# Loading x and memory by features and moving 1/rms behind the product in a two-layer encoder trunk

## The chip, the cores and the metric

One core of one Trainium2 chip runs the whole program. The metric is device time in microseconds (us) of one execution; three executions of the kernel before are given.

## The reference, cut to what matters

Two sequences of 256 tokens with 1024 features each, and 256 memory tokens for each, go through two layers. All is fp32.

```python
def rms_norm(x, g):
    xf = x.astype(jnp.float32)
    y = xf * lax.rsqrt(jnp.mean(xf * xf, axis=-1, keepdims=True) + EPS)
    return (y * g.astype(jnp.float32)).astype(x.dtype)

# per layer i (0: differential attention, 1: dilated windows)
h = rms_norm(x, norm_mix[i])
kv = (rms_norm(mem, norm_mem[i]) @ w_mem_kv[i]).reshape(B, M, 2, X_HEADS, X_HEAD_DIM)
mk = rms_norm(kv[:, :, 0], xk_norm[i])
mv = kv[:, :, 1]
p = h @ w_in                     # queries, keys: rms_norm by head, rope; values as they are
xq = rms_norm(p[..., -X_WIDTH:].reshape(B, S, X_HEADS, X_HEAD_DIM), xq_norm[i])
cross = memory_attention(xq, mk, mv).reshape(B, S, X_WIDTH)
x = x + jnp.concatenate([mixed, cross], axis=-1) @ w_out
x = x + conv_ffn(rms_norm(x, norm_ffn[i]), w_up[i], conv_w[i], conv_b[i], w_down[i])
```

The root of the mean of squares is one number for each token (row of x or mem). It multiplies a whole row, so it commutes with the product by the weights. Behind the product, queries and keys are normed by head again, where a row's factor cancels but for the place of EPS.

## The kernel before, in words

The 512 tokens of the two sequences are four token tiles of 128 (NT = 4). A product of fp32 accuracy is made of three matmuls of rounded parts (`mm3`, lines 370 to 373: high by high, low weights by high, high weights by low), so each operand is split in a high part (`hh`, `wh`) and a low part (`hl`, `wl`). Weights come as units of 128 x 1024 (512 KB), in the order of a list: `w_loader` (L333) issues the load of each on SyncE's queue into one of three buffers `raw`, and `w_splitter` casts it on ACT (L348) and subtracts on DVE (L350) into one of six pairs `wh`, `wl`. `next_unit` hands the units to the products.

TensorE contracts over the partitions, so the operand must lie with features on partitions, and x and mem are loaded with tokens on them. `norm_transposed` (L391) therefore takes a token tile: ACT sums squares (L381), POOL adds EPS and takes the power -1/2 (L386, L387), then the first half of the row is multiplied by root and gain on DVE (L403) and the second by the root on ACT (L406) and by the gain on POOL (L408). Four TensorE transpositions of 128 x 128 a half (L415) go to a bank `tp`, and `evac_split` writes the high part on ACT (L428) and the low part on DVE (L430). `norm_h` does so for x, into `hh` and `hl`; `mem_tiles` for memory, into buffers `blk`. For layer 1 the transposition also permutes the tokens (`perm_fwd`).

`proj_first` (L526) is the first product, eight feature blocks by four token tiles for 512 columns, in the order of the list `FIRST`, which visits tiles as they come. It keeps one PSUM bank for each of the tiles (three `acc`, one `sc`). `fan_out` hands a finished bank's two halves to their posts: `qk_post` (L552: squares on ACT, sums on DVE, root on POOL by L572 and L573, scaling on DVE L577, rope on POOL L589 to L592, transposition on PE L605) or `v_post` (L618, a copy on ACT). The second product makes queries and keys of attention pair 0; then comes `mem_proj` (L678), keys and values of memory, token tile by token tile with all four weight units of it. Pairs' attention (`attn_a`) and the cross attention run beside the products. In layer 0's FFN, the down projection goes in two passes over column halves, and the memory product of layer 1 follows the second.

The order of instructions on each engine is not written out: every stage is a Python generator, and a planner in the program (`Sched`, with a cost for each operation and a queue of events by planned time) runs them and so issues the instructions in planned order. The chip then keeps each engine's order and waits by semaphores.

Two lines matter for the start. `load_x` is called with units X0_U and X1_U, and `start` sends x's first tile, then the gain, the identity, and the first unit.

Of the kernel before, what the change touches and what calls it, by code (L numbers as in the profile page):

```python
# [31 lines left out]
X0_U, X1_U = 1, 3  # L32
FIRST = [(0, 0), (1, 0), (0, 1), (1, 1), (2, 0), (2, 1), (0, 2), (1, 2), (2, 2), (3, 0), (3, 1), (3, 2), (0, 3), (1, 3), (2, 3), (3, 3)]
X_AT = (1, 2, 3)
# [227 lines left out]
def trunk_kernel(ctx: ExitStack, tc: tile.TileContext, io: dict, out: bass.AP):  # L262
# [7 lines left out]
    psum = ctx.enter_context(tc.tile_pool(name="psum", bufs=1, space=bass.MemoryType.PSUM))  # L270

# [31 lines left out]
    const.tile([128, 64], F32, name="spacer")  # L303
    X = const.tile([128, NT, D], F32, name="X")
    x_ready = []
    dma_t = [2.0]

    def dma(eng, out_, in_, nbytes):
        eng.dma_start(out_, in_)
        dma_t[0] += nbytes / 330e3  # L310
        return dma_t[0]

    mask = tail.tile([128, 2, 512], BF16, name="mask")
    subg = tail.tile([128, 128], F32, name="subg")
    convT = tail.tile([128, 2, 4, 2 * NFF], F32, name="convT")
# [17 lines left out]
    def w_loader():  # L333
        for u in range(len(plan)):
            for t in X_AT[0:1] if u == X0_U else X_AT[1:] if u == X1_U else ():
                load_x([t])
# [40 lines left out]
    def row_scale(src, h):  # L377

        ss = sm(2, "ss")
        for j in range(2):  # L380
            nc.scalar.activation(h[j].v, src[j], AF.Square, scale=1.0 / 32, accum_out=ss[:, j:j + 1])  # L381
            t = S.op("ACT", c_act(512, 0, 1))
        yield t
        rstd = sm(1, "rstd")
        s1 = sm(1, "s1")
        nc.gpsimd.tensor_scalar(s1, ss[:, 0:1], ss[:, 1:2], EPS, ALU.add, ALU.add)  # L386
        nc.gpsimd.tensor_tensor(rstd, s1, mhalf[:, 0:1], ALU.pow)  # L387
        yield S.op("POOL", 0.6)
        return rstd

    def norm_transposed(src, gkey, ident_, evac, src_done=None):  # L391

        g = gains[gkey]
        h = []
        for _ in range(2):
            b = yield from qn_s.get()
            h.append(b)
        rstd = yield from row_scale(src, h)
        finished = [S.event(), S.event()]

        def part(j):
            if j == 0:
                nc.vector.scalar_tensor_tensor(h[0].v, src[0], rstd, g[0].v, ALU.mult, ALU.mult)  # L403
                t = S.op("DVE", c_dve(512, 1))
            else:
                nc.scalar.activation(h[1].v, src[1], AF.Copy, scale=rstd)  # L406
                yield S.op("ACT", c_act(512, 1))
                nc.gpsimd.tensor_tensor(h[1].v, h[1].v, g[1].v, ALU.mult)  # L408
                t = S.op("POOL", c_pool(512))
            if src_done:  # L410
                src_done(j, t)
            yield t
            tp = yield from tp_s.get()
            for k in range(4):
                nc.tensor.transpose(tp.v[:, k * 128:k * 128 + 128], h[j].v[:, k * 128:k * 128 + 128], ident_)  # L415
                t = S.op("PE", T_PE)
            h[j].done(t)
            yield t
            yield from evac(j, tp)
            finished[j].set(S.now)  # L420

        S.spawn(part(1))
        S.spawn(part(0))
        for f in finished:
            yield f
# [13 lines left out]
    def norm_h(t, gkey, permuted, x_ev, h_ev):  # L439
# [18 lines left out]
        yield from norm_transposed([X[:, t, 0:512], X[:, t, 512:1024]], gkey, perm_fwd if permuted else ident, evac)  # L458
# [992 lines left out]
```

## Time and profile before

| | |
|---|---|
| executions | 1428.8, 1430.7, 1432.24 us (median 1430.7) |
| profiled execution | 1430.49 us |
| its span | 1428.5 us, granted clock 1.00 |
| TensorE busy | 1399.0 us, 98% |
| VectorE, ScalarE, GpSimd busy | 783.7, 622.1, 340.2 us |
| chain that ended last | PE 87%, POOL 5%, DVE 3% |
| DMA | 129.31 MB, mean 91 GB/s |

The span runs from the first to the last recorded instruction; the execution's time has a further 2 us around it. Busy times of matmuls are modelled: they are pipelined, so a row's duration (0.39 us at full speed) is longer than the distance to the next. Starts tell the pace. TensorE is the only engine that is nearly always busy; the places where it stands are what the lists of waits show.

### The profile page before, as it was taken

To read this page: it belongs to the slowest core of one execution; us is meant where nothing else is said; L and a number is where in the kernel's file an instruction comes from. 1 tells how busy PE (TensorE), PEld (TensorE's weight loads), DVE (VectorE), ACT (ScalarE), POOL (GpSimd) and SP (SyncE) were. 2 spreads that over 40 slices of the span, in tenths; PEclk is the share of its full clock that TensorE was granted. 3 is DMA by queue.
4 is the path that set the end of the run, shared out by engine and by line. 5 is a ranking of instruction groups with operands and counts; after the bars stand their busy time and mean duration, and the time that the engine had idled before them with its cause. 6 is when DMAs were issued, how large, how long until landed. Compare 5 with 4: busy or idle time off the path is not lost.

```text
span 1428.5 us, 18859 instructions
## 1 busy us (share of the span) xinstructions
PE 1399.0 (98%) x7168; PEld 1163.6 (81%) x7168; DVE 783.7 (55%) x1218; ACT 622.1 (44%) x1145; POOL 340.2 (24%) x652
## 2 busy tenths in 40 slices
PE   6999999999999999999999999999999999999999
PEld 4778788879888888878878888888889888888887
DVE  5576657876664366445664334344476663466353
ACT  5566555535442244244446534454454442243231
POOL 5834665121000000030164165445130000000000
PEclk9999999999999999999999999999999999999999
DMA  6421231123333333423221311222222323333221
GB/s 224 150 74 46 62 116 60 60 74 105 106 100 95 97 103 90 136 100 133 74 89 29 96 68 59 60 63 77 83 87 91 103 92 100 97 95 103 89 74 59
DMA packets 39258, 129.31 MB, mean 91 GB/s; under 512 B 4608, under 2 KB 5504, under 8 KB 39168
## 3 DMA queue, kind: packets, MB, share of 16 engines
q1 hardware_dynamic: 39168, 128.11, 28.6%
q8 instruction: 56, 0.92, 0.3%
q14 instruction: 34, 0.28, 0.1%
HBM read 126.00 MB, written 2.10 MB: 90 GB/s over the span
## 4 chain that ended last, share of the span: by engine, by line
PE 87%; POOL 5%; DVE 3%; issue 2%; DMA 2%; ACT 1%; SPq 0%; POOLq 0%; DVEq 0%; ACTq 0%
PE acc L371 17%; PE acc L373 17%; PE acc L372 17%; PE sc L371 7%; PE sc L372 7%; PE sc L373 7%; PE sc L784 3%; PE tp L707 2%; PE o L982 2%; POOL rstd L573 2%; PE tp L605 1%; DMA raw<-w 1%; PE o L371 1%; PE o L372 1%; PE o L373 1%
## 5 line engine op out<-in xcount | busy, mean ns | idle before, releaser
L350 DVE TENSOR_TENSOR wl<-raw,wh 128x1024 fp32r<-128x1024 f32 x220 | 273.7, 1247 | 244.9 <-ACT wh L348 243.7
L348 ACT CAST wh<-raw 128x1024 fp32r<-128x1024 f32 x220 | 231.2, 1053 | 369.7 <-PE sc L372 187.9
L371 PE MATMUL acc<-wh,hh 128*128 128x512 f32 (+1 forms) x536 | 216.6, 404 | 0.8 <-ACT hh L428 0.8
L373 PE MATMUL acc<-wh,hl 128*128 128x512 f32 (+1 forms) x536 | 203.7, 380 | 0.0
L372 PE MATMUL acc<-wl,hh 128*128 128x512 f32 (+1 forms) x536 | 203.4, 379 | 0.0
L371 PE MATMUL acc<-wh,blk 128*128 128x512 f32 x368 | 149.1, 405 | 0.0
L372 PE MATMUL acc<-wl,blk 128*128 128x512 f32 x368 | 143.6, 390 | 0.0
L373 PE MATMUL acc<-wh,blk 128*128 128x512 f32 x368 | 143.6, 390 | 0.0
L371 PE MATMUL acc<-hh,wh 128*128 128x512 f32 (+1 forms) x384 | 143.2, 373 | 0.0
L371 PE MATMUL sc<-hh,wh 128*128 128x512 f32 (+1 forms) x384 | 142.8, 372 | 0.0
L372 PE MATMUL acc<-hl,wh 128*128 128x512 f32 (+1 forms) x384 | 142.6, 371 | 0.0
L373 PE MATMUL sc<-hh,wl 128*128 128x512 f32 (+1 forms) x384 | 142.6, 371 | 0.0
L372 PE MATMUL sc<-hl,wh 128*128 128x512 f32 (+1 forms) x384 | 142.6, 371 | 0.0
L373 PE MATMUL acc<-hh,wl 128*128 128x512 f32 (+1 forms) x384 | 142.6, 371 | 0.0
L371 PEld LDWEIGHTS acc<-wh,hh 128*128 128x128 f32 x536 | 101.9, 190 | 20.7 <-issue 5.3
L373 PEld LDWEIGHTS acc<-wh,hl 128*128 128x128 f32 x536 | 101.2, 189 | 19.9 <-DVE hl L430 0.3
L372 PEld LDWEIGHTS acc<-wl,hh 128*128 128x128 f32 x536 | 101.7, 190 | 14.1 <-DVE wl L350 0.5
L386 POOL TENSOR_SCALAR s<-ss 128x1 f32<-128x1 f32 x24 | 11.4, 475 | 425.6 <-ACT qn L381 419.8
L573 POOL TENSOR_TENSOR rstd<-ss,mhalf 128x4 f32<-128x4 f32 x96 | 105.5, 1099 | 8.0
L567 DVE TENSOR_REDUCE ss<-sq 128x4 f32<-128x256 f32 x96 | 39.8, 415 | 88.0 <-ACT sq L564 87.6
L373 PEld LDWEIGHTS acc<-hh,wl 128*128 128x128 f32 x384 | 72.3, 188 | 12.6
L371 PEld LDWEIGHTS acc<-hh,wh 128*128 128x128 f32 x384 | 72.3, 188 | 12.5
(145 smaller groups left out, 2412.3 us busy)
## 6 DMA issues: line engine op xcount, KB each, us to landing
raw<-w SPq DMA_DIRECT2D x220, 512.0 KB, 3.6
blk<-mem SPq DMA_DIRECT2D x16, 256.0 KB, 6.6
y<-X SPq DMA_DIRECT2D x8, 256.0 KB, 2.0
X<-x SPq DMA_DIRECT2D x3, 512.0 KB, 9.7
blk<-norm_mix SPq DMA_DIRECT2D x4, 256.0 KB, 7.0
blk<-norm_mem SPq DMA_DIRECT2D x4, 256.0 KB, 5.5
blk<-norm_ffn SPq DMA_DIRECT2D x4, 256.0 KB, 5.1
X<-x SPq DMA_DIRECT2D x2, 256.0 KB, 3.2
```

The costliest lines, as they stand in the source:

```text
L348: nc.scalar.copy(hi.v, r.v)
L350: nc.vector.tensor_tensor(lo.v, r.v, hi.v.bitcast(F32), ALU.subtract)
L371: nc.tensor.matmul(out_, ah, bh, start=start, stop=False)
L372: nc.tensor.matmul(out_, ah, bl, start=False, stop=False)
L373: nc.tensor.matmul(out_, al, bh, start=False, stop=stop)
L386: nc.gpsimd.tensor_scalar(s1, ss[:, 0:1], ss[:, 1:2], EPS, ALU.add, ALU.add)
L567: nc.vector.tensor_reduce(ss, sq.v[:, 0:256].rearrange("p (a d) -> p a d", d=64), AX.X, ALU.add)
L573: nc.gpsimd.tensor_tensor(rstd, ss, mhalf[:, 0:4], ALU.pow)
L605: nc.tensor.transpose(tp.v[:, x * 128:x * 128 + 128], src[:, x % 2, b * 128:b * 128 + 128], ident)
L707: nc.tensor.transpose(tp.v[:, i * 128:i * 128 + 128], e.v[:, i * 128:i * 128 + 128], ident)
L784: nc.tensor.matmul(sc[h].v[:, c:c + n], q.v[half(h), tq], k.v[half(h), ks], start=True, stop=True)
L982: nc.tensor.matmul(o[:, t, h, :], eT.v[:, i * 128:i * 128 + 128], vt[s].v[:, c:c + 64], start=(i == 0), stop=(i == 3))
```

## The change

x of layer 0 and memory of both layers are also handed over transposed by the host (`xT`, `memT`: features on partitions) and loaded as eight blocks of 128 features by 512 tokens. The norm's gain is then one number a partition, `gT`, and goes into the split (`split_feature`): ACT multiplies and rounds the high part, DVE subtracts. No transposition is made there. x and mem are loaded by rows too, for the sums of squares alone; `row_stats` leaves for each token tile the root and EPS times (mean square + EPS), `nr`. The second is the EPS of the norm by head in `qk_post` (a pointer in place of a constant), the first scales values in `v_post`. For layer 1's x, whose tokens are permuted by the transposition, these numbers are written to DRAM and read back in the new order (`permuted_stats`), and `norm_h` multiplies by the gain alone, both halves on DVE. The other norms (before the FFNs) keep root and gain, both halves on DVE. `proj_first` goes feature by feature over the four token tiles, and for the last unit tile by tile.

```diff
@@ the split and the statistics @@
+    def permuted_stats(s):
+        for i in range(2):
+            yield here[2 * s + i]
+        for i in range(2):
+            nc.sync.dma_start(nrmd[s][128 * i:128 * i + 128, :], nrmx[:, 2 * s + i, :])
...
+        for j in range(2):
+            for y in range(2):
+                nc.sync.dma_start(nrms[64 * y:64 * y + 64, 2, 2 * s + j, :], rows[2 * j + y])
...
+    def row_stats(key, src, done=None):
+        ss = yield from mean_squares(src, done)
+        m = sm(1, "s1")
+        eps, rstd = nr[key]
+        if key[0] == "x1":
+            eps, rstd = nrmx[:, key[1], 0:1], nrmx[:, key[1], 1:2]
+        nc.gpsimd.tensor_scalar(m, ss[:, 0:1], ss[:, 1:2], EPS, ALU.add, ALU.add)
+        nc.gpsimd.tensor_scalar(eps, m, EPS, None, ALU.mult)
+        nc.gpsimd.tensor_tensor(rstd, m, mhalf[:, 0:1], ALU.pow)
...
+    def split_feature(raw, g, hi, lo):
+        nc.scalar.activation(hi, raw, AF.Copy, scale=g)
+        nc.vector.scalar_tensor_tensor(lo, raw, g, hi.bitcast(F32), ALU.mult, ALU.subtract)
@@ norm_h @@
+            if permuted:
+                nc.vector.tensor_tensor(h[j].v, src[j], g[j].v, ALU.mult)
+            else:
+                nc.vector.scalar_tensor_tensor(h[j].v, src[j], rstd, g[j].v, ALU.mult, ALU.mult)
@@ proj_first @@
-        for u, t in FIRST:
...
+        for u in range(4):
+            wh, wl, done = yield from next_unit(name, 2)
+            order = [(k, t) for k in range(2) for t in range(NT)]
+            for k, t in order if u < 3 else sorted(order, key=lambda x: x[1]):
+                kk = 2 * u + k
+                yield k_evs[kk]
...
+                if kk == KD - 1:
+                    fan_out(t, bks[t], posts)
@@ qk_post, v_post @@
+            yield nr_ev[key, t]
-            nc.gpsimd.tensor_scalar(ss, ss, 1.0 / 64, EPS, ALU.mult, ALU.add)
+            nc.gpsimd.tensor_scalar(ss, ss, 1.0 / 64, nr[key, t][0], ALU.mult, ALU.add)
-            nc.scalar.copy(vs[s].val.v[:, 256 * i:256 * i + 256], ps)
+            nc.scalar.activation(vs[s].val.v[:, 256 * i:256 * i + 256], ps, AF.Copy, scale=nr[key, t][1])
@@ mem_tiles, mem_proj @@
+        for k in range(KD):
+            raw = yield from blk.get()
+            nc.sync.dma_start(raw.v, io["memT"][:, k, :])
+            landed = S.now + 4.0
...
+            yield landed
+            yield from split_feature(raw.v, gT[:, 1 + 3 * l, k:k + 1], hi.v, lo.v)
...
+            if k == 1:
+                S.spawn(rows())
...
+                    yield mT[kk]
+                    hi, lo = mT[kk].val
@@ the start @@
+    with_unit = {1: [lambda: load_xT(2), lambda: load_xT(3)], 2: [lambda: load_xT(4), lambda: load_xT(5)],
+                 3: [lambda: load_xT(6), lambda: load_xT(7)],
+                 4: [lambda: S.spawn(setup())] + [lambda t=t: load_x(t) for t in range(2)],
+                 5: [lambda t=t: load_x(t) for t in range(2, 4)]}
...
+        nc.sync.dma_start(gT, io["gT"])
+        load_xT(0)
+        yield 0.001
+        load_xT(1)
```

The planner moves more than the diff says. First, the start of TensorE's queue (`acc`, `tp` are PSUM banks, the number behind a name is the allocation). Before:

```order
L415 MATMUL tp_128<-ident,qn_115 128x128 x4
L415 MATMUL tp_137<-ident,qn_116 128x128 x4
L371 MATMUL acc_159<-wh_107,hh 128x512
L372 MATMUL acc_159<-wl_108,hh 128x512
L373 MATMUL acc_159<-wh_107,hl 128x512
L371 MATMUL acc_159<-wh_107,hh 128x512
L372 MATMUL acc_159<-wl_108,hh 128x512
L373 MATMUL acc_159<-wh_107,hl 128x512
L415 MATMUL tp_170<-ident,qn_142 128x128 x4
```

After:

```order
L366 MATMUL acc_99<-wh_113,hh 128x512
L367 MATMUL acc_99<-wl_114,hh 128x512
L368 MATMUL acc_99<-wh_113,hl 128x512
L366 MATMUL acc_100<-wh_113,hh 128x512
L367 MATMUL acc_100<-wl_114,hh 128x512
L368 MATMUL acc_100<-wh_113,hl 128x512
L366 MATMUL acc_101<-wh_113,hh 128x512
L367 MATMUL acc_101<-wl_114,hh 128x512
L368 MATMUL acc_101<-wh_113,hl 128x512
```

The transpositions are gone, and each weight tile is used for all four token tiles in turn, where before one tile ran ahead with the features at hand.

Second, TensorE's queue in the first token tile of layer 0's memory product (its bank is `acc_808` before, `acc_730` after; `blk` are the split features; `sc`, `e`, `eT`, `o` are scores, weights, transposed weights and outputs of attention pair 0). Before:

```order
L415 MATMUL tp_814<-ident,qn_768 128x128 x4
L371 MATMUL acc_808<-wh_457,blk_618 128x512
L372 MATMUL acc_808<-wl_458,blk_618 128x512
L373 MATMUL acc_808<-wh_457,blk_619 128x512
L415 MATMUL tp_832<-ident,qn_769 128x128 x4
L371 MATMUL acc_808<-wh_474,blk_618 128x512
L372 MATMUL acc_808<-wl_475,blk_618 128x512
L373 MATMUL acc_808<-wh_474,blk_619 128x512
L371 MATMUL acc_808<-wh_474,blk_618 128x512
```

After, from feature 5's three matmuls to feature 6's first; right above it stand feature 4's three matmuls, eight transpositions of queries (L644) and four scores (L813):

```order
L366 MATMUL acc_730<-wh_683,blk_767 128x512
L367 MATMUL acc_730<-wl_684,blk_767 128x512
L368 MATMUL acc_730<-wh_683,blk_768 128x512
L813 MATMUL sc_839<-blk_785,blk_587 128x256
L813 MATMUL sc_852<-blk_785,blk_587 128x256
L813 MATMUL sc_839<-blk_797,blk_614 128x256
L813 MATMUL sc_852<-blk_797,blk_614 128x256
L736 MATMUL tp_858<-ident,e_825 128x128 x2
L736 MATMUL tp_863<-ident,e_828 128x128 x2
L914 MATMUL o_815<-blk_508,eT_857 128x128 x2
L914 MATMUL o_815<-blk_508,eT_862 128x128 x2
L366 MATMUL acc_730<-wh_699,blk_818 128x512
```

Scores, transpositions of weights and outputs of pair 0, which stood among the matmuls of its later tiles and behind, now stand between the features of its first tile.

Third, SyncE's queue ahead of layer 1's memory product (`raw` is a weight unit, `memT` a feature block, `mem` half a tile by rows). Before:

```order
L323 DMA blk_5584<-norm_mem 128x512
L324 DMA blk_5585<-norm_mem 128x512
L653 DMA blk_5590<-mem 128x512
L653 DMA blk_5592<-mem 128x512
L653 DMA blk_5594<-mem 128x512
L653 DMA blk_5596<-mem 128x512
L653 DMA blk_5598<-mem 128x512
L653 DMA blk_5600<-mem 128x512
L653 DMA blk_5602<-mem 128x512
L653 DMA blk_5604<-mem 128x512
L338 DMA raw_5620<-w 128x1024
```

After, from feature 3 on:

```order
L696 DMA blk_5634<-memT 128x512
L690 DMA blk_5650<-mem 128x512
L690 DMA blk_5652<-mem 128x512
L333 DMA raw_5664<-w 128x1024
L333 DMA raw_5687<-w 128x1024
L696 DMA blk_5689<-memT 128x512
L690 DMA blk_5700<-mem 128x512
L690 DMA blk_5702<-mem 128x512
L696 DMA blk_5710<-memT 128x512
L690 DMA blk_5721<-mem 128x512
L690 DMA blk_5723<-mem 128x512
L696 DMA blk_5727<-memT 128x512
```

And ACT's queue at the same place, after:

```order
L377 ACTIVATE sq_5616,ss<-blk_5592 128x512
L343 CAST wh_5620<-raw_5523 128x1024
L343 CAST wh_5668<-raw_5561 128x1024
L424 ACTIVATE blk_5636<-blk_5634,gT 128x512
L377 ACTIVATE sq_5683,ss<-blk_5650 128x512
L377 ACTIVATE sq_5683,ss<-blk_5652 128x512
```

Before, the memory's loads were issued as one block ahead of the weight units; now features 4 to 7 stand behind two units, and the split of feature 3 (L424) behind the casts of two (L343).

## Rows read from the trace of the kernel before

**Rows 1.** The page: busy us, share of the span and instructions of each engine.
```profile
PE 1399.0 (98%) x7168; PEld 1163.6 (81%) x7168; DVE 783.7 (55%) x1218; ACT 622.1 (44%) x1145; POOL 340.2 (24%) x652
```

**Rows 2.** List of waits, PE: waiting tile and line <- releaser: us, times, longest.
```profile
PE tp L415 <- DMA ident<-c_ident: 9.4, 1, 9.4
PE tp L415 <- DVE qn L403: 6.5, 9, 1.3
PE tp L605 <- POOL qn L592: 4.1, 4, 1.9
```

**Rows 3.** Table of stretches; columns: us, busy of five engines, PEclk, DMA share, GB/s.
```profile
9.44:43.96 34.52, 30.42 (x128) 23.11 (x129) 23.78 (x38) 20.76 (x39) 24.97 (x59) 1.00 0.53 179
43.96:72.95 28.99, 26.54 (x130) 20.94 (x128) 14.09 (x26) 15.85 (x34) 24.29 (x50) 1.00 0.51 184
72.95:107.81 34.86, 33.62 (x185) 26.11 (x184) 25.74 (x52) 22.51 (x60) 12.28 (x19) 1.00 0.23 74
601.08:649.80 48.72, 47.72 (x225) 38.99 (x224) 22.10 (x30) 22.67 (x42) 13.92 (x18) 1.00 0.34 110
```

**Rows 4.** Timeline of ACT, start: start us, us, line, operation, tile, idle before, releaser.
```profile
3.81 0.63 ACT L381 ACTIVATE qn<-X 128x512 f32<-128x512 f32 x1 [1.81 <-DMA X<-x]
...
10.87 1.04 ACT L348 CAST wh<-raw 128x1024 fp32r<-128x1024 f32 x1 [3.90 <-DMA raw<-w]
```

**Rows 5.** Table of stretches, three microseconds at the start, columns as in rows 3.
```profile
9.00:12.00 3.00, 2.20 (x8) 1.43 (x8) 0.05 (x1) 1.13 (x2) 1.27 (x1) 1.00 1.01 407
```

**Rows 6.** Timeline of PE in the first product.
```profile
14.42 0.63 PE L371 MATMUL acc<-wh,hh 128*128 128x512 f32 x1
14.85 0.63 PE L372 MATMUL acc<-wl,hh 128*128 128x512 f32 x1
...
18.68 0.40 PE L372 MATMUL acc<-wl,hh 128*128 128x512 f32 x1
...
35.80 0.39 PE L371 MATMUL acc<-wh,hh 128*128 128x512 f32 x1
...
43.96 0.39 PE L371 MATMUL acc<-wh,hh 128*128 128x512 f32 x1
```

**Rows 7.** Timeline of POOL behind the first product.
```profile
36.93 0.19 POOL L572 TENSOR_SCALAR ss<-ss 128x4 f32<-128x4 f32 x1 [1.54 <-DVE ss L567]
...
44.54 1.24 POOL L591 TENSOR_TENSOR ropew<-qn,rope_aq 128x32 f32<-128x32 f32 x1
...
52.55 0.30 POOL L386 TENSOR_SCALAR s<-ss 128x1 f32<-128x1 f32 x1
...
54.42 0.24 POOL L591 TENSOR_TENSOR ropew<-qn,rope_aq 128x32 f32<-128x32 f32 x1
...
58.66 0.32 POOL L592 TENSOR_TENSOR qn<-ropew 128x64 f32<-128x64 f32 x1
```

**Rows 8.** Timeline of PE: query and norm transpositions.
```profile
52.97 0.33 PE L605 MATMUL tp<-ident,qn 128*128 128x128 f32 x1 [0.35 <-DVE qn L577]
...
84.15 0.60 PE L415 MATMUL tp<-ident,qn 128*128 128x128 f32 x4
84.58 0.60 PE L605 MATMUL tp<-ident,qn 128*128 128x128 f32 x4
```

**Rows 9.** Timeline of DVE: softmax of the first attention pair.
```profile
88.28 1.28 DVE L765 TENSOR_REDUCE mn<-sc 128x2 f32<-128x512 f32 x2
...
91.32 0.17 DVE L871 RECIPROCAL r<-ssum 128x2 f32<-128x2 f32 x1 [0.77 <-ACT e L772]
...
92.11 0.48 DVE L875 SCALAR_TENSOR_TENSOR e<-e,r 128x256 f32<-128x256 f32 x1
```

**Rows 10.** DMA issues: operation, count, KB each, median us from issue to landing.
```profile
raw<-w SPq DMA_DIRECT2D x220, 512.0 KB, 3.6
blk<-mem SPq DMA_DIRECT2D x16, 256.0 KB, 6.6
...
X<-x SPq DMA_DIRECT2D x3, 512.0 KB, 9.7
```

More of the change, by code (lines that the diff above doesn't have):

```diff
@@ L383, in row_scale @@
         yield t
[L384 to L425, printed above, removed]
@@ new lines, in row_stats @@
+    def row_stats(key, src, done=None):
[7 more added lines that the diff above has]
+        nc.gpsimd.tensor_tensor(rstd, m, mhalf[:, 0:1], ALU.pow)
+        yield S.op("POOL", 1.1)
+        if key[0] == "x1":
+            here[key[1]].set(S.now)
+        else:
+            nr_ev[key].set(S.now)
@@ L456, in evac, with part @@
             yield from evac_split(tp, v, dv(hh), dv(hl), 512)
-        yield from norm_transposed([X[:, t, 0:512], X[:, t, 512:1024]], gkey, perm_fwd if permuted else ident, evac)
+        g = gains[gkey]
+        src = [X[:, t, 0:512], X[:, t, 512:1024]]
+        h = []
+        for _ in range(2):
+            b = yield from qn_s.get()
+            h.append(b)
+        if permuted:
+            S.spawn(row_stats(("x1", t), src))
+        else:
+            ss = yield from mean_squares(src)
+            rstd = sm(1, "rstd")
+            s1 = sm(1, "s1")
+            nc.gpsimd.tensor_scalar(s1, ss[:, 0:1], ss[:, 1:2], EPS, ALU.add, ALU.add)
+            nc.gpsimd.tensor_tensor(rstd, s1, mhalf[:, 0:1], ALU.pow)
+            yield S.op("POOL", 0.6)
+        finished = [S.event(), S.event()]
+        def part(j):
+            if permuted:
+                nc.vector.tensor_tensor(h[j].v, src[j], g[j].v, ALU.mult)
+            else:
+                nc.vector.scalar_tensor_tensor(h[j].v, src[j], rstd, g[j].v, ALU.mult, ALU.mult)
+            yield S.op("DVE", c_dve(512, 1))
+            tp = yield from tp_s.get()
+            for k in range(4):
+                nc.tensor.transpose(tp.v[:, k * 128:k * 128 + 128], h[j].v[:, k * 128:k * 128 + 128],
+                                    perm_fwd if permuted else ident)
+                te = S.op("PE", T_PE)
+            h[j].done(te)
+            yield te
+            yield from evac(j, tp)
+            finished[j].set(S.now)
+        S.spawn(part(0))
+        S.spawn(part(1))
+        for f in finished:
+            yield f
         h_ev.set(S.now)
@@ L464, in go @@
         def go():
-            if start is not None:
+            if start:
                 yield start
@@ L469, in go @@
             parts = [S.event() for _ in range(NT)]
+            if permuted:
+                for s in range(2):
+                    S.spawn(permuted_stats(s))
             def one(i):
@@ L642, in mem_tiles, with rows @@
     def mem_tiles(l, evs):
-        t = yield from load_gain(("mem", l), io["norm_mem"][l])
-        loaded = [S.event() for _ in range(NT)]
-        def load():
-            for i in range(NT):
+        def rows():
+            for t in range(NT):
                 m = []
@@ L1329, in main @@
         cross = [ev(), ev()]
[L1330 to L1331 removed]
+        mT = [ev() for _ in range(KD)]
+        halves = [qk_post(None, gc(G_XQ[0], G_XQ[0]), "x0", xq)]
         outs = []
```

178 lines of the change are left out of this document (86 added, 92 removed).

## The prediction

> **What bounds the kernel now.** I read the busy table first: TensorE (PE) works 1399.0 of 1428.5 us [rows 1]. So only two things can pay: fewer PE instructions, or fewer of the 29.5 us in which PE stands. The list of PE's waits says where those lie [rows 2]: 9.4 us ahead of the first transposition, 6.5 us at norm transpositions that wait for VectorE (DVE), 4.1 us at transpositions of queries and keys that wait for GpSimd (POOL). Third came the table by stretches [rows 3]: PE is idle for 4.1 us in the first product (9.44 to 43.96), 2.45 in the second (to 72.95), 1.24 in the memory product (to 107.81), 1.0 in the last pass of layer 0's down projection with the memory product of layer 1. Behind those stretches nothing waits for long, so time won or lost in one of them stays won or lost. The other engines matter only where their chain comes out later than PE's place in its fixed order.
>
> The sum is made against the profiled execution's 1430.49 us (span 1428.5 plus 2.0 outside it), which stands 0.2 below the median 1430.7. About 0.2% (2.9 us) is what a measurement here can tell from no change.
>
> **Part 1, the start and the first product.** Removed: 32 transpositions (8 groups of four) and the wait for identity, rows, squares and gain ahead of them. Added: 8 splits by feature, the same two passes over 512 columns that a transposed tile needed. Before, the first 256 KB had landed when ScalarE (ACT) took them at 3.81, and unit w0 (the first 512 KB of weights) when ACT cast it at 10.87 [rows 4]. Queued up to and with w0 were then 1.6 MB (X tile 0, the gain on all partitions, identity, w0): 1.35 MB in 7.06 us, or 191 KB per us. Now it is gT, two features and w0: 1.05 MB, 0.79 MB behind the first 256 KB. At that rate w0 lands at 3.81 + 4.1 = 7.9; at the 407 GB/s of 9 to 12 us [rows 5], at 5.7. I take 7.2, nearer the slow end, since half rows like the features' are what moved slowly then. ACT's cast of 1.04 [rows 4] and DVE's subtraction of the same tile follow (1.25, estimated a fifth above the cast), so the product runs without a break from 9.5.
>
> Its 96 matmuls go at the pace of 35.80 to 43.96, where 36 took 8.16 us, 0.227 each [rows 6]: 21.8 us. But at 14.42 and 14.85 the pace is 0.43 [rows 6], which is the level of 1.2 GHz, though the clock column reads 1.00 there; by 18.68 a matmul lasts 0.40 and no longer 0.63, the level of 2.4 GHz. The low level lasted 4.3 us from the first unbroken matmuls, or 9.2 from the first transposition at 9.4 [rows 2]. At 0.43 for 0.227, 47% of such time is lost: 2.0 to 4.3 us; I take 2.9, between them. First product's end: 9.5 + 21.8 + 2.9 = 34.2 for 43.96, **-9.8 us** (-11.7 with w0 at 5.7 and the short warming, -7.7 with both late). The features, x by rows and the next units are due later than w0 by 5 us and more each, at 5.4 us of matmuls a unit; I cost them at nothing, covered by that lead. If it is gone, PE waits at a feature.
>
> **Part 2, the second product.** POOL's first reciprocal root for the first product's halves came at 36.93 [rows 7], 7.0 us ahead of the product's end, because token tile 0 was complete early. Now all four tiles end together, 1.36 us apart (six matmuls), so POOL starts 3.0 us ahead of the end: 4.0 us later against PE. The chain is eight pairs of a short sum and a power, with four ropes; a pointer in place of a constant in the sum costs about 0.1 (0.30 against 0.19 in POOL's rows [rows 7]), 0.9 for eight. Before, the fourth transposition of the cross queries waited 0.35 and ran at 52.97 [rows 8], 9.0 behind the product's end; the last rope ended at 58.66 + 0.32 [rows 7], 15.0 behind it. Now these data are there 13.4 and 19.9 behind the end. Without stalls the stretch takes 28.99 less 2.45 of idle less 4 groups of norm transpositions at 0.43 (84.15 to 84.58 [rows 8]): 24.8. PE reaches the two places 8.2 and, after the first stall, 17.6 behind the end: stalls of 5.2 and 2.3. That makes 32.3 for 28.99, **+3.3 us** (0 to +5: at 0 POOL's long forms shrink, see below). X's statistics for the pointer come from loads behind unit 3, some ten microseconds ahead of the first use: nothing, unless the queue stalls.
>
> **Part 3, the memory product of layer 0.** Removed: 4 groups of transpositions, 1.7 us. The order of PE's instructions shows the new price: between feature 4 and features 5 to 7 of token tile 0, PE's queue now holds pair 0's eight transpositions, all four sets of scores, weight transpositions and most outputs, with six matmuls among them. What hid the softmax before was 72 matmuls in between; here PE waits for it. A set's chain on DVE: two minima, 1.28, and twice the 1.27 from reciprocal to subtraction (91.32 to 92.11 + 0.48) [rows 9], 3.8 in all, plus what ACT's exponentials and the splits of features push in: 4.3. Timing from the second product's end: 15 matmuls 3.4; the wait for the last rope of the keys until 6.8 (POOL is behind there already: 4.1 us of waits before [rows 2]); transpositions and scores until 8.4; four sets, 25.6; features 5 to 7, 26.4. Tiles 1 to 3 take 72 matmuls, 16.3, and 2.9 of attention: 45.6 for 34.86. Some 2.5 us of that is attention that no longer stands later (8 scores, 8 output matmuls and 4 weight transpositions more than before). **+8.2 us** (+3 where sets overlap down to 3.0, +11 where the features' splits fall into the chain).
>
> The stalls here are short ones, a few microseconds each. The longest wait of PE after the start is 1.9 us in this trace [rows 2], and behind it the matmuls keep their pace; so by the rows a stall costs only itself. The Trainium skill, "TensorE: Matmul & The Clock Gate", section "HAM oscillation — how this bites in real kernels", says otherwise for longer gaps: there the array falls back to its low clock and must warm again. No run here shows such a gap, and my sum leaves it out; it is a rival below.
>
> **Part 4, the memory product of layer 1.** Removed: 8 groups, 3.4 us, and 1.0 of waits in the 48.72 us of [rows 3]. Added: features in place of rows, loaded one at a time. Four of them stand on SyncE's queue (SP) behind two weight loads that wait for DVE's splits of buffers that the pass itself still reads; feature 3's split on ACT stands behind a cast that waits for the pass's last matmul. So features 4 to 7 are issued about 2.8 to 6.5 us behind the pass's end. A 512 KB unit lands 3.6 after issue and a memory tile 6.6 when eight are queued [rows 10]; with 4.8 between, the last lands at 11.3, its split and the row squares among them bring it to 13.4, and tile 0 is done at 14.1 instead of 5.4. 48.72 - 4.4 + 8.7 = 53.0, **+4.2 us** (+2.5 with 3.6 to landing, +6 with 6.6).
>
> **Part 5, the three later norms.** The permuted norm of layer 1 multiplies by the gain alone, so its transpositions don't wait for the root, and POOL's multiplication of half a tile is gone from all three. Of the 6.5 us at norm transpositions [rows 2] some 3 are in these; DVE gets the second half instead. I take **-1.0** (-2 to 0). The statistics go through DRAM, a write and a read, and are needed only when the layer's first product is complete, some 18 us behind; two transfers of 3.6 [rows 10] and a POOL chain make 12. Hidden by 6 us. Gains, casts and values (a scale in place of a copy on ACT) move no PE work: nothing, as ACT and DVE have slack behind PE there.
>
> **Sum**: -9.8 + 3.3 + 8.2 + 4.2 - 1.0 = +4.9, so 1430.49 + 4.9 = 1435.4 us. The first and the later terms have one cause: less PE work early brings PE sooner to places where others set the pace.
>
> **The rivals.**
> 1. *Not slower, because POOL is not late.* The same POOL multiplication lasted 0.24 at 54.42 and 1.24 at 44.54 [rows 7]; the long forms may come from sharing with DVE, and may be rare in the new order. Four ropes at 1.4 for 2.4 save 4 us: part 2 falls to 0, the keys' rope is ready when PE comes, and part 3 to +5.2. Sum -1.4, 1429.1; with an early w0 as well (-11.7) 1427.2. For it: of the rows shown, two ropes' multiplications differ by 1 us with the same operands. Against: the pairs alone keep POOL behind. It decides where the cross queries' transpositions wait under 1.5 us. Chance 0.35, more than half of it faster by over 2.9 us (1424 if the sets overlap too).
> 2. *The clock falls in the stalls.* Some four gaps (cross queries, keys, the sets, layer 1's features), and 4.3 us of low level behind each, 47% lost [rows 6]: 2.0 each, +8 with part of it inside waits, +6 taken: 1441.4. By the rule of the Trainium skill named in part 3 it would go so; the trace has no gap to show it. Chance 0.2.
> 3. *The change does not free layer 1's statistics in time.* If each DRAM step takes 9.7 us, as the X tiles' loads did [rows 10], 2 x 9.7 + 5 is 24 for 18: another +6, 1441. Chance 0.05.
>
> **How the numbers follow.** Forecast 1435.4, chance 0.4 with its own range 1431 to 1440. Slower by over 0.2% means above 1433.6: 0.28 of the forecast's 0.4 and all of rivals 2 and 3: 0.53. Within: 0.10 of the forecast and 0.15 of rival 1: 0.25. Faster: 0.02 of the forecast and 0.20 of rival 1: 0.22. The range from 1425 (rival 1, early w0) to 1444 (rival 2 with part 3 at its upper end) leaves out 2 in 10.
>
> **What would show it.** Right, if the first product ends at 33 to 36; if PE's waits list new rows at query transpositions for POOL or DVE and at scores or outputs for ACT and DVE, 10 us or more between the second product's end and the end of memory tile 0; and feature waits of some 8 us near 625. Step 1 falls if w0 lands after 8.5, step 3 if tile 0 ends within 20 us of the second product's end. The whole is wrong if PE's waits sum to less than 40 us: PE loses about 10.3 us of transpositions (24 groups at 0.43), so only more idle time than 29.5 + 10.3 makes it slower.

## The result and the profile after

The changed kernel takes 1440.9 us (median of 4 runs, 1440.42 to 1441.9) against 1430.22 of before: a ratio of 1.0075, 95% interval 1.0057 to 1.0092. It is slower, as forecast; 1440.9 lies in the range of 1425 to 1444, 5.5 us above the forecast 1435.4. The profiled execution took 1441.29 us with a span of 1439.2. The page's first part, beside [rows 1]:

```profile
PE 1398.5 (97%) x7072; PEld 1162.1 (81%) x7072; DVE 773.6 (54%) x1218; ACT 616.8 (43%) x1121; POOL 315.4 (22%) x644
```

TensorE has 96 instructions fewer, yet is busy as long as before: a part of its work went slower. The list of PE's waits (waiting tile and line <- releaser: total us, times, longest), beside [rows 2]:

```profile
PE acc L366 <- ACT wh L343: 9.6, 1, 9.6
PE acc L366 <- DVE qn L616: 8.2, 1, 8.2
PE tp L644 <- POOL qn L631: 7.6, 5, 2.3
PE acc L366 <- ACT blk L424: 5.6, 3, 3.9
PE sc L813 <- ACT blk L648: 2.2, 2, 1.7
```

Two entries are new and large: 8.2 us at one matmul that waits for DVE's scaling of queries, and 5.6 us at matmuls that wait for a memory feature on ACT. The table of stretches, cut where the products begin and end in this trace, beside [rows 3] (us of the stretch, busy of PE, weight loads, DVE, ACT and POOL, then granted clock, DMA share, GB/s):

```profile
9.60:34.05 24.45, 23.98 (x96) 19.18 (x96) 15.57 (x27) 17.43 (x32) 11.72 (x30) 1.00 0.77 283
34.05:70.45 36.40, 27.14 (x113) 21.71 (x113) 16.12 (x31) 16.42 (x33) 30.87 (x73) 0.86 0.46 150
70.45:99.90 29.45, 23.83 (x100) 15.40 (x98) 18.01 (x41) 18.75 (x55) 8.29 (x20) 0.77 0.36 132
70.45:120.36 49.91, 43.10 (x194) 31.10 (x193) 29.68 (x65) 28.38 (x75) 16.36 (x30) 0.86 0.22 79
608.27:661.83 53.56, 47.45 (x193) 37.31 (x192) 19.83 (x27) 21.76 (x38) 9.23 (x18) 0.90 0.40 129
```

The first product ends at 34.05 where it ended at 43.96. The second takes 36.40 for 28.99, the memory product of layer 0 takes 49.91 for 34.86 (29.45 of it in token tile 0), the last pass with layer 1's memory product 53.56 for 48.72. The clock column, 1.00 in every row of before, reads 0.86, 0.77 and 0.90 in the last four. In three-microsecond pieces it comes down to half speed, the level of 1.2 GHz (the first piece holds the moment of the fall):

```profile
37.00:40.00 3.00, 0.00 (x0) 0.00 (x0) 1.35 (x3) 0.57 (x2) 2.70 (x8) 0.67 0.55 202
82.00:85.00 3.00, 2.75 (x8) 1.34 (x7) 2.12 (x6) 1.99 (x9) 0.00 (x0) 0.50 0.04 14
639.00:642.00 3.00, 1.83 (x4) 0.79 (x3) 0.75 (x1) 2.90 (x8) 1.64 (x3) 0.50 0.76 292
```

It fell in the gap behind the first product (8.15 us long), in the waits around pair 0's first scores, and in the gap at layer 1's feature 4 (3.95 us). On PE's timeline the first of them reads:

```profile
33.82 0.39 PE L368 MATMUL sc<-wh,hl 128*128 128x512 f32 x1
42.36 0.77 PE L366 MATMUL acc<-wh,hh 128*128 128x512 f32 x1 [8.15 <-DVE qn L616]
42.93 0.63 PE L367 MATMUL acc<-wl,hh 128*128 128x512 f32 x1
...
47.62 0.63 PE L366 MATMUL acc<-wh,hh 128*128 128x512 f32 x1
...
48.38 0.40 PE L368 MATMUL acc<-wh,hl 128*128 128x512 f32 x1
48.62 0.40 PE L366 MATMUL acc<-wh,hh 128*128 128x512 f32 x1
```

The first matmul behind the gap waited 8.15 us for DVE, and from there to 47.62 the pace is 0.43 instead of 0.227.

Both kernels issue the same 5568 product matmuls, in nearly the same order, so the start of the same matmul in the two timelines gives a ledger of where time went. Shifts against the kernel before, in us (plus is later), of all runs:

| product matmul | changed | e1 | e2 | e3 | e4 | e5 | e6 | e7 | e8 | e9 | e10 |
|---|---|---|---|---|---|---|---|---|---|---|---|
| 97th, first of the second product | -1.6 | -2.6 | -8.7 | -2.7 | -2.6 | -7.0 | -6.2 | -10.9 | +0.6 | -9.9 | +1.7 |
| 193rd, first of memory, layer 0 | -2.5 | -2.0 | -5.5 | -1.7 | +0.6 | -8.8 | -6.2 | -8.0 | -1.9 | -5.6 | -1.0 |
| 289th, behind that product | +12.6 | +10.4 | +10.5 | -5.5 | +3.3 | +5.7 | -9.9 | -11.4 | -5.3 | -6.1 | +16.9 |
| 385th | +9.7 | +7.6 | +7.7 | -5.2 | +2.8 | +2.9 | -10.7 | -11.2 | -5.3 | -5.7 | +14.0 |
| 1151st, layer 0's FFN | +7.2 | +5.1 | +5.2 | -7.3 | +0.8 | +0.4 | -10.5 | -12.8 | -7.5 | -8.3 | +11.5 |
| 2401st, first of memory, layer 1 | +3.0 | +0.9 | +1.1 | -11.4 | +0.4 | -3.8 | -14.7 | -17.0 | -11.6 | -8.8 | +7.4 |
| 2501st, behind that product | +12.0 | +8.8 | +9.6 | -12.6 | +0.4 | +6.1 | -15.8 | -18.1 | -12.8 | -8.8 | +17.4 |
| 5561st, near the end | +10.5 | +7.3 | +8.0 | -11.6 | +0.5 | +4.6 | -16.3 | -19.6 | -13.4 | -10.3 | +15.9 |

For the changed kernel: the first product ends 9.9 earlier; the second gives back 7.4; the memory product costs 15.1, of which 3.1 come back by the 700th matmul; layer 0's FFN norm gains 2.2; the last pass with layer 1's memory product costs 4.8; layer 1's two norms gain 1.4.

Why did the second product wait? Its first matmul needs the PSUM bank of token tile 0, which both halves' posts must have read, and POOL held them up (POOL's timeline: last statistics of x, last of twelve multiplications for layer 1's rope tables, first pair of the query norm):

```profile
34.41 0.57 POOL L415 TENSOR_TENSOR nrms<-s,mhalf 128x1 f32<-128x1 f32 x1
...
36.91 0.22 POOL L1344 TENSOR_TENSOR rope_b<-blk 128x16 f32<-128x16 f32 x1
37.24 0.27 POOL L611 TENSOR_SCALAR ss<-ss,nrms 128x4 f32<-128x4 f32 x1
37.59 1.02 POOL L612 TENSOR_TENSOR rstd<-ss,mhalf 128x4 f32<-128x4 f32 x1
...
40.74 1.01 POOL L612 TENSOR_TENSOR rstd<-ss,mhalf 128x4 f32<-128x4 f32 x1
```

A pair is the short sum (L611) and the power (L612) that give the root for one half of a finished bank. POOL's first pair began at 37.24, 3.2 us behind the product's end, where the forecast had it 3.0 ahead: rope tables that layer 1 needs stand ahead of it, and more between the pairs. In the kernel before it began at 36.93 [rows 7]. So the first product came 9.9 us earlier, and POOL's queue did not. At layer 1 the queue of SyncE and ACT's casts read as forecast; ACT's timeline (a cast that waits for the pass, then a feature that waits for its load):

```profile
630.23 1.06 ACT L343 CAST wh<-raw 128x1024 fp32r<-128x1024 f32 x1 [4.39 <-PE sc L368]
631.18 0.72 ACT L424 ACTIVATE blk<-blk,gT 128x512 fp32r<-128x512 f32 x1
...
636.93 0.72 ACT L424 ACTIVATE blk<-blk,gT 128x512 fp32r<-128x512 f32 x1 [3.66 <-DMA blk<-memT]
```

### The profile page after: what moved, and what is told of

The parts are those of the page before. It is cut to its first block, busy times and chain, and to the rows that moved or that the text cites. A ratio compares the mean times of both kernels' runs of the same rounds, so it can differ in the third digit from the quotient of the medians.

```text
span 1439.2 us, 18651 instructions
## 1 busy us (share of the span) xinstructions
PE 1398.5 (97%) x7072; PEld 1162.1 (81%) x7072; DVE 773.6 (54%) x1218; ACT 616.8 (43%) x1121; POOL 315.4 (22%) x644
## 4 chain that ended last, share of the span: by engine, by line
PE 90%; POOL 5%; DMA 2%; issue 1%; ACT 1%; DVE 1%; SPq 0%; POOLq 0%; ACTq 0%
PE acc L366 18%; PE acc L368 18%; PE acc L367 18%; PE sc L366 7%; PE sc L368 7%; PE sc L367 7%; PE sc L813 3%; PE tp L736 2%; PE o L1011 2%; POOL rstd L612 2%; PE tp L644 1%; PE o L367 1%; PE o L366 1%; PE o L368 1%; PE o L844 1%; PE o L914 1%
## 5 line engine op out<-in xcount | busy, mean ns | idle before, releaser
L345 DVE TENSOR_TENSOR wl<-raw,wh 128x1024 fp32r<-128x1024 f32 x220 | 268.9, 1229 | 256.7 <-ACT wh L343 255.8
L343 ACT CAST wh<-raw 128x1024 fp32r<-128x1024 f32 x220 | 230.9, 1051 | 381.7 <-PE sc L367 188.0
L366 PE MATMUL acc<-wh,blk 128*128 128x512 f32 x368 | 150.4, 409 | 5.6 <-ACT blk L424 5.6
L368 PE MATMUL acc<-wh,blk 128*128 128x512 f32 x368 | 145.4, 395 | 0.9 <-DVE blk L426 0.9
L612 POOL TENSOR_TENSOR rstd<-ss,mhalf 128x4 f32<-128x4 f32 x96 | 103.9, 1083 | 8.0
L413 POOL TENSOR_SCALAR s<-ss 128x1 f32<-128x1 f32 x16 | 7.5, 471 | 378.1 <-ACT sq L377 377.6
L366 PEld LDWEIGHTS acc<-wh,blk 128*128 128x128 f32 x368 | 70.1, 191 | 20.7 <-ACT blk L424 7.0
L616 DVE TENSOR_TENSOR qn<-acc,rstd 128x256 f32<-128x256 f32 x94 | 39.8, 423 | 85.6 <-POOL rstd L612 83.4
```

The costliest lines, as they stand in the source:

```text
L343: nc.scalar.copy(hi.v, r.v)
L345: nc.vector.tensor_tensor(lo.v, r.v, hi.v.bitcast(F32), ALU.subtract)
L366: nc.tensor.matmul(out_, ah, bh, start=start, stop=False)
L368: nc.tensor.matmul(out_, al, bh, start=False, stop=stop)
L612: nc.gpsimd.tensor_tensor(rstd, ss, mhalf[:, 0:4], ALU.pow)
L616: nc.vector.tensor_tensor(v, ps.rearrange("p (h d) -> p h d", d=64), rstd.unsqueeze(2).to_broadcast([128, 4, 64]), ALU.mult)
```

## The experiments

The question was which of these costs are waits of their own and which the clock's, what made each wait, and whether x or memory is to blame. Two theories ran through them: *order* (loading one feature at a time and leaving POOL's tables where they are puts waits into TensorE's order) and *clock* (the fall to 1.2 GHz behind the waits makes the loss).

| run | median us | before beside it | ratio, 95% interval |
|---|---|---|---|
| changed | 1440.9 | 1430.22 | 1.0075 (1.0057 to 1.0092) |
| e1_fill | 1437.43 | 1430.8 | 1.0044 (1.0029 to 1.0059) |
| e2_tiles | 1440.07 | 1430.8 | 1.0067 (1.0050 to 1.0083) |
| e3_ahead | 1418.94 | 1430.8 | 0.9916 (0.9901 to 0.9931) |
| e4_xonly | 1430.64 | 1430.8 | 0.9994 (0.9985 to 1.0003) |
| e5_late | 1434.72 | 1431.55 | 1.0022 (1.0012 to 1.0031) |
| e6_ahead_late | 1413.67 | 1431.55 | 0.9879 (0.9862 to 0.9895) |
| e7_ahead_late_tiles | 1412.03 | 1431.55 | 0.9872 (0.9852 to 0.9892) |
| e8_memory_only | 1417.26 | 1431.55 | 0.9902 (0.9886 to 0.9918) |
| e9_x_late_tiles | 1420.67 | 1432.41 | 0.9919 (0.9901 to 0.9937) |
| e10_memory_serial | 1445.17 | 1432.41 | 1.0087 (1.0063 to 1.0111) |

The runs stand in four groups, each with the kernel before beside it (medians 1430.22 to 1432.41). Between groups it is the ratios that compare; differences of a microsecond or two between times of different groups tell nothing.

**e1_fill: the gaps filled with idle matmuls.**

```diff
+    def fill(n, slots_):
+        b = yield from slots_.get()
+        for _ in range(n):
+            nc.tensor.matmul(b.v, hh[:, 0, 0:128], hh[:, 0, 0:512], start=True, stop=True)
+        b.done(S.now)
...
         yield from proj_first("a_w_in", halves[0:2], k_evs)
+        yield from fill(34, tp_s)
...
+                    if l == 1 and t == 0 and 4 <= kk < 7:
+                        yield from fill((18, 8, 5)[kk - 4], tp_s)
```

> The changed kernel with matmuls that nobody reads put on TensorE where it stands: 34 behind the first product (7.7 of the 8.15 us gap), 10 and 9 at the two waits ahead of pair 0's first scores, 18, 8 and 5 ahead of features 4 to 6 of layer 1's memory product. The order of all other work is the same; the results are those of the changed kernel. Theory 'clock' (the fall to 1.2 GHz behind each wait is a good part of the loss): the granted clock stays 1.00, the stretch 42 to 48 us gains up to 2.7 us, memory tile 0 of layer 0 takes 23 to 26 instead of 29.4 us, the last tile gains 1.4: 1433 to 1437 us. Theory 'waits alone' (DVE's softmax chain and POOL set the pace, as the prediction had it): tile 0 still takes 26.4 or more, and what is gained at 42 us is lost again at the next POOL wait: 1439 to 1441.

Measured 1437.43, 3.5 us under the changed kernel. Memory tile 0 in e1:

```profile
70.92:98.00 27.08, 24.44 (x119) 16.55 (x117) 18.19 (x42) 18.91 (x56) 8.29 (x20) 0.94 0.38 145
```

It takes 27.08 for 29.45, at a mean clock of 0.94 for 0.77. The gain at the second product (97th matmul 1.0 earlier, then at full pace) was gone by its end, where the 193rd matmul stands 0.5 later than in the changed kernel: a transposition now waited 2.9 us for DVE's scaling, behind POOL, and the clock fell there instead (mean 0.57 from 52 to 60 us). So neither theory has it all. Filling the gaps gave back 3.5 of the 10.7 us (4.1 against before), most of it in layer 0's memory tile 0. That is an estimate of the clock's cost from below, as the clock still reads 0.50 for 10.2 us of e1 behind the start, against 34.1 in the changed kernel. With most of the fall gone that tile took 27.1 where the prediction, which left the clock out, had 26.4.

**e2_tiles: token tile 0 complete earlier.** The last two weight units of the first product go by tiles.

```diff
-            for k, t in order if u < 3 else sorted(order, key=lambda x: x[1]):
+        for u in range(3):
+            order = [(u, k, t) for k in range(2) for t in range(NT)]
+            if u == 2:
+                order = sorted(order + [(3, k, t) for k in range(2) for t in range(NT)], key=lambda x: x[2])
+            for v, k, t in order:
```

> The changed kernel with the last two weight units of the first product (not the last alone) taken token tile by token tile, so that tile 0 is complete 8.2 us ahead of the product's end as before, instead of 4.1. Theory 'late tiles' (the 8.15 us gap comes from tile 0's late end): the gap falls by about 4 us, to 4, the second product ends 4 or more us earlier, and the whole takes 1434 to 1437. Rival 'POOL's queue' (rope tables and x's statistics stand ahead of the first pair and hold it until 37 us whatever the tiles do): the gap stays at 7 or more, 1440 to 1441.

1440.07: the 8.15 us gap became 1.18, less than even the first theory had it, but the time is the rival's, nearly that of the changed kernel. On PE's timeline of e2:

```profile
35.31 0.47 PE L366 MATMUL acc<-wh,hh 128*128 128x512 f32 x1 [1.18 <-DVE qn L623]
...
45.91 0.75 PE L366 MATMUL acc<-wh,hh 128*128 128x512 f32 x1 [4.88 <-DVE qn L623]
```

The second bank's matmul now waited 4.88. Of 7.1 us that the 97th matmul came earlier than in the changed kernel, 3.0 were left at the second product's end and 2.1 behind the memory product. The profiled execution keeps 2.5 us, but it is the fastest of its four; the medians differ by 0.8. Most of the gap had only moved to a later wait on the same chain.

**e3_ahead: three features in flight instead of one.**

```diff
+        for _ in range(3):
+            yield from load()
         for k in range(KD):
-            raw = yield from blk.get()
-            nc.sync.dma_start(raw.v, io["memT"][:, k, :])
-            landed = S.now + 4.0
+            raw, landed = ring[k]
...
-            if k == 1:
+            if len(ring) < KD:
+                yield from load()
+            if k == KD - 1:
                 S.spawn(rows())
```

> The changed kernel with three memory features in flight instead of one, for both layers, and the memory rows for the statistics behind the last feature. TensorE's order then has no attention between the features of memory tile 0. Theory 'serial loading put the attention in the gap': the memory product of layer 0 falls from 49.9 to 36 to 39 us (some 3 of it come back later, as the attention stands later again), that of layer 1 from 31.8 to 23 to 26: 1422 to 1429. Rival 'features are late anyway' (their loads stand behind weight units on SyncE's queue, so TensorE waits for features instead): 1435 or more.

1418.94: more than expected, and 0.84% faster than before. Memory product of layer 0, and last pass with layer 1's:

```profile
71.28:102.28 31.00, 31.00 (x165) 24.15 (x164) 19.15 (x44) 21.18 (x58) 11.99 (x27) 1.00 0.40 134
593.79:637.30 43.51, 43.51 (x193) 36.04 (x192) 19.16 (x25) 18.95 (x33) 4.77 (x10) 1.00 0.46 146
```

PE is busy through both, at a clock of 1.00: 31.00 us for 49.91, 43.51 for 53.56. Some of the first is attention that stands later again; by matmul number e3 is 14.9 us ahead of the changed kernel at the 385th and 22.1 at the 5561st. The list of waits, in which the features no longer stand, shows what is left:

```profile
PE acc L366 <- DVE qn L616: 7.8, 1, 7.8
PE tp L644 <- POOL qn L631: 4.6, 4, 2.1
PE tp L644 <- DVE qn L616: 3.3, 3, 2.2
```

**e4_xonly: memory by rows as before, the rest of the change kept.**

```diff
-            nc.sync.dma_start(raw.v, io["memT"][:, k, :])
...
+                    nc.sync.dma_start(b.v, io["mem"][:, i, 512 * j:512 * j + 512])
...
+            yield from norm_transposed([x.v for x in m], ("mem", l), ident, evac, lambda j, te: m[j].done(te))
```

> Memory by rows with transpositions in both layers, as in the kernel before; the rest of the change kept. Ledger of the traces by matmul number: the change's memory parts cost 15.0 - 2.8 and 4.8 us. If each part costs by itself, what is left is -9.9 at the start, +7.4 in the second product, -3.7 in the norms: 1424 us. Rival (the late POOL chain of the first product runs on into whatever stands behind it, so that memory by rows would be late too, its norms needing POOL): +3 to +6 more, 1427 to 1432.

1430.64, the time of before: the rival. The start's 10.2 us are lost by the 193rd matmul, at +0.6, and the memory product loses another 2.7, its norms waiting for POOL:

```profile
PE acc L366 <- DVE qn L667: 7.4, 1, 7.4
...
PE tp L467 <- POOL qn L460: 4.5, 4, 2.6
```

So the memory part of the change, with its features loaded one at a time, costs 10.3 us net (1440.9 - 1430.64), and x by features in this form gives nothing.

**e5_late: layer 1's rope tables later on POOL.**

```diff
             tab = ropes[key]
+            if key == "b0":
+                yield S.now + 40.0
```

> The changed kernel with layer 1's rope tables (24 short POOL multiplications, due only in layer 1) written 40 us later in the plan; nothing else is edited. In the changed kernel's trace 12 of them stand between x's last statistics (34.98) and the first pair of the first product's halves (37.24) and 12 more between the next pairs. Theory 'POOL's queue': the first pair moves from 37.2 to about 35, the gap at the second product falls from 8.15 to about 4, the second product ends 3 to 4 us earlier: 1436 to 1438 us. Rival 'only the late end of token tile 0' (sums of the first half ready at 32.5, but the second half and the bank later anyway): gap 7 to 8, 1440 to 1441.

1434.72, 6.2 us under the changed kernel, more than the theory had. In its POOL timeline the statistics end at 32.59 and the pairs follow each other:

```profile
32.03 0.56 POOL L415 TENSOR_TENSOR nrms<-s,mhalf 128x1 f32<-128x1 f32 x1
32.70 1.10 POOL L611 TENSOR_SCALAR ss<-ss,nrms 128x4 f32<-128x4 f32 x1
33.88 1.02 POOL L612 TENSOR_TENSOR rstd<-ss,mhalf 128x4 f32<-128x4 f32 x1
35.01 0.27 POOL L611 TENSOR_SCALAR ss<-ss,nrms 128x4 f32<-128x4 f32 x1
```

PE's first matmul of the second product ran at 36.98 for 42.36, and the product ended 6.3 us earlier than in the changed kernel. The last statistics end 2.4 us earlier than in the changed kernel too, since four of the tables' multiplications had stood ahead of them. So the gap hangs on where the first pairs stand in POOL's queue. Either edit alone brings them ahead of most tables: e2 by an earlier tile (its first pair runs at 30.87), e5 by later tables. In e2 statistics and tables then stand behind the first two pairs and hold up the next bank; in e5 they don't, and the gain stays until the product's end.

**e6_ahead_late and e7_ahead_late_tiles: the remedies together.** Their diffs are those of e3, e5 and, in e7, e2.

> Three features in flight and the late rope tables together. With the attention out of memory tile 0, nothing behind the second product should give back what POOL's shorter queue saves. Theory 'POOL's queue': 3 to 4 us under the kernel with features ahead alone (1418.9): 1415 to 1416. Rival (the next POOL chain, the keys' ropes, sets the pace there): 1418 to 1419.

> As the run before, and with the last two weight units of the first product by token tiles. Tiles alone took the gap at the second product from 8.15 to about 1.5 us but gave only 3 of these at its end, as POOL was late for the transpositions. With POOL freed of the tables the rest should come: second product's end at 63 to 65 us, 1412 to 1415. Rival: POOL's eight pairs and eight ropes set the end whatever stands beside them: 1415 to 1419.

1413.67 and 1412.03. The late tables give 5 to 6 us on top of e3 (5.3 by the times, 6.0 against before), more than expected; tiles give 1.6 more, which the two intervals don't separate. In the profiled executions the 193rd matmul is at -6.2 and -8.0. e7 is the fastest kernel here, 1.28% under before. What is left of its waits:

```profile
PE acc L366 <- ACT wh L343: 7.8, 1, 7.8
PE tp L651 <- POOL qn L638: 5.4, 5, 2.1
PE tp L651 <- DVE qn L623: 3.3, 2, 2.8
PE acc L366 <- ACT blk L424: 2.3, 1, 2.3
```

**e8_memory_only: x of layer 0 by rows, memory features three in flight.**

```diff
-        yield from proj_first("a_w_in", halves[0:2], k_evs)
+        yield from proj_first("a_w_in", halves[0:2], h0)
```

The first product, its order, the loads of x and the norm ahead of it are those of before; the posts of its halves take EPS as a constant.

> x of layer 0 by rows with transpositions and the first product in the order of before (with no factor behind the product there); memory by features, three in flight, and layer 1's x as in the change. If the memory parts carry the gain of the kernel with features ahead: layer 0's memory product loses 1.7 us of transpositions and layer 1's 3.4 with its 1.0 of waits, the later norms give 3.7: 1420 to 1422 us. If the start is needed for it (the changed start minus 9.9, given back by 7.4 in the second product in the changed kernel): 1424 or more.

1417.26, better than expected, and its interval overlaps that of e3, which has x by features as well: memory alone carries the whole gain of e3.

**e9_x_late_tiles: x alone, with POOL's queue mended.** e4's diff with those of e5 and e2.

> Memory by rows as before; x by features with the late rope tables and the last two units by token tiles. By matmul number x by features alone (run e4_xonly) won 10.2 us up to the first product's end and had lost it again at the second's. If that loss is POOL's queue and the late tile, as the runs with features ahead have it, most of it comes back: 1422 to 1426 us. Rival (the memory norms, which then need POOL too, take it): 1428 to 1431.

1420.67: x by features is worth 10 us and more once POOL's first pairs come early (1430.64 for e4, 1432.41 for before). The first matmul of the second product keeps the start's 9.9 us; 4.3 of it go until the 193rd, in waits for DVE's scalings and for POOL, the longest 1.81 us. The two parts do not add up: x alone won 11.7 us against before, memory alone (e8) 14.3, both together (e7) 19.5.

**e10_memory_serial: memory one feature at a time, x as before.** e8's diff without e3's.

> x of layer 0 by rows and the first product as before; memory by features one at a time as in the change; layer 1's x as in the change. Theory 'serial loading alone makes the loss': memory tile 0 of layer 0 still has the attention between its features and takes 25 to 30 us, layer 1's waits stay: 1434 to 1441 us. Rival (it needs the hurried start of the x part, which brings TensorE to the memory product before the features): under 1430.

1445.17, above the range given; by the ratios it is not told apart from the changed kernel. Memory tile 0, with the waits of the whole run:

```profile
72.00:104.71 32.71, 22.56 (x101) 14.85 (x100) 19.10 (x43) 20.33 (x61) 9.03 (x21) 0.79 0.36 125
```

```profile
PE tp L652 <- POOL qn L639: 9.3, 5, 3.8
...
PE acc L369 <- ACT blk L427: 6.4, 4, 4.2
PE tp L747 <- DVE e L915: 3.4, 2, 3.2
```

It takes 32.7 us at a clock of 0.79, without any hurry at the start. Against e8, which differs in the loads in flight alone, serial loading costs some 27 us. It makes the loss by itself.

## Why the prediction was right, and where it was off

The direction and the two causes (attention between the features of memory tile 0, features behind weight units in layer 1) were right; the forecast +4.9 became +10.7. Part 2 fell short by 4.1 us and part 3 by 3.8, and part 5 hid 2.7 of that. Rival 2, the falling clock, stood nearest to the number with its 1441.4, but by chance: the clock was not all of the difference. By the steps:

- *Part 1, forecast -9.8, measured -9.9.* The end at 34.05 is the forecast's 34.2, by two errors that cancel: the product ran without a break from its second matmul at 10.86 and not from 9.5, as w0 landed later, and the low level cost 1.7 and not 2.9 us (10.86 + 95 x 0.227 + 1.7 is 34.1). ACT's cast of w0 waited for the load until 8.50, the limit that the prediction had set for this step. w0's landing moves by itself: the first matmul waits until 7.8 in e7 and 9.6 here, with the same loads ahead of it.
- *Part 2, forecast +3.3, measured +7.4.* The step that failed is "X's statistics for the pointer come from loads behind unit 3 ... nothing, unless the queue stalls", with "POOL starts 3.0 us ahead of the end". POOL began 3.2 behind it, since the last statistics ended at 34.98 and twelve rope-table multiplications followed. I had looked at POOL's posts and not at the setup work that the change moves onto them. The wait came at the bank of the first matmul, not at the query transpositions, and 13 matmuls at half pace came behind it (2.6 us). With the tables moved (e5) the product ended 6.3 us earlier, so POOL's queue was the cause for the larger part.
- *Part 3, forecast +8.2, measured +15.1 less 3.1.* The order was read rightly: tile 0 took 29.45 for 26.4, and e1 puts 2.4 of the 3.1 over the forecast to the clock. What the sum had mis-sized is the clock at nothing. Tiles 1 to 3 took 20.5 for 19.2. The wait that was named, for DVE's softmax chain, did not show. These are the stretches of the changed kernel up to the last score of the first set and from there to feature 7, the latter in e1, and DVE's minima, with which a set's chain begins:

```profile
70.45:82.18 11.73, 7.16 (x32) 4.49 (x31) 4.55 (x6) 6.47 (x12) 6.00 (x15) 0.86 0.90 329
82.18:99.15 16.97, 15.95 (x69) 10.63 (x67) 12.71 (x34) 11.53 (x39) 1.79 (x5) 0.69 0.00 2
81.63:96.98 15.35, 13.31 (x68) 8.83 (x67) 12.62 (x34) 11.42 (x39) 1.79 (x5) 0.89 0.04 14
82.28 1.29 DVE L794 TENSOR_REDUCE mn<-sc 128x2 f32<-128x512 f32 x2 [1.09 <-PE sc L813]
86.42 1.37 DVE L794 TENSOR_REDUCE mn<-sc 128x2 f32<-128x512 f32 x2
93.17 1.29 DVE L794 TENSOR_REDUCE mn<-sc 128x2 f32<-128x512 f32 x2 [1.19 <-PE sc L813]
```

The first stretch took 11.7 us for the forecast's 8.4. The second took 17.0 for the 17.2 of four sets at 4.3, but by two errors that cancel: only three sets' chains stand ahead of feature 7, and each took some 5.7. TensorE stood idle for only 1.0 us of the second stretch; the other 4.6 of tile 0's waits came in the first, for the keys' rope and the copies behind it. By these rows (busy matmul time is modelled) TensorE was at work on the attention itself, in part at half speed, and DVE in turn waited for scores. With more of the clock (e1) the three sets still took 15.35 us. Which engine sets their pace stays open.

- *Part 4, forecast 53.0, measured 53.56.* The product waited 5.6 us for high parts of features and 0.6 for a low one, and 13 matmuls behind at half pace cost 2.6, on 44.3 without any. The sum is right within its range, in part by luck: its 8.7 us were waits alone, and 6.2 of waits with 2.6 of the clock came to the same. (53.0 less 48.72 is +4.3, not the +4.2 of the sum.)
- *Part 5, forecast -1.0, measured -3.7* (2.2 and 1.4). In the trace of before TensorE's waits at the transpositions of these three norms sum to 3.3 us, 1.8 of them for DVE's half and 1.5 for DVE's low parts, none for POOL; of the 6.5 us in [rows 2] they hold 1.8, not "some 3". In the changed kernel the list has no wait at these transpositions. So nearly all of them went, where the sum took a third.
- *Rivals.* Rival 1 was wrong: POOL's short forms were common, and it was late all the same. Its sign came (the fourth transposition of the cross queries waited 0.11 us), since the wait stood at the bank ahead of it. The range's lower end, 1425, is below its own sum of 1427.2. Rival 2 came true, at some 3.5 to 4 us by e1 (from below) and not +6: in the second product the full pace had won 1.0 us at the first matmul and nothing by the end. By the rule of the Trainium skill, "TensorE: Matmul & The Clock Gate", section "HAM oscillation — how this bites in real kernels", a gap brings the low clock back; this trace agrees, with the clock at 0.50 from within the gaps of 8.15 and 3.95 us. It shows more: in memory tile 0 the clock fell behind waits of 2.33 and 1.73 us, and in e7, whose mean is 0.998, once behind one of 2.76. Rival 3 fell: the statistics were read back from DRAM with issues at 726.70, and POOL's first use at 737.60 waited 0.74 for DVE's sums, not for them.
- *The signs.* The first product ended at 34.05, within 33 to 36; TensorE's idle time, 1439.2 less 1398.5, is 40.7 us, just over the 40 asked for; the waits for features near layer 1's memory product were 6.2 us for some 8. The waits between the second product's end and the end of tile 0 were 5.6 us where 10 or more were to show.

The chance of 0.53 for slower was fair; the price was too low, by POOL's queue and by the clock.

## What to carry to other kernels

When a planner serializes loads by an assumed landing time, it fills the pause with whatever is at hand, and on the chip that filler, with its own work and waits, stands in front of what was due: three loads in flight instead of one turned +10.7 into -11.9 us here. When work is taken off the busiest engine's start, look for what else stands in the next engine's queue there (here rope tables of another layer) and move it. Count a gap on TensorE with its clock: filling it with idle matmuls tells in one run what the clock takes at least, if the clock column then shows how much of the fall is gone.

## What the runs showed that was not expected

- The clock column of before reads 1.00 at 14.42 although matmuls run at 0.43 us each; behind the changed kernel's gaps it reads 0.50 at the same pace. The traces' first clock records begin at 18.13 in before and at 14.13 in the changed kernel, where the pace rises, and the column reads 1.00 where there is no record. At the start the pace, not the column, tells the level.
- Short POOL work can hold TensorE for much longer than it lasts, because one PSUM bank hangs on the pairs behind it. The 24 multiplications of layer 1's rope tables last 0.22 us each in most cases; moving them (e5) brought the first matmul of the second product 5.4 us forward.
